# Two encoder layers on one core: the Fourier branch on even and odd halves, gates and branch products with channels on partitions, h scaled ahead of its transposes, tokens in natural order

## The chip, the cores and the metric

The kernel runs on one core of a Trainium2 chip. The metric is the device time of one execution in microseconds. The core has a matrix engine (TensorE, PE), a vector engine (DVE), a scalar engine (ACT), GpSimd (POOL), a queue engine for transfers (SyncE, SP), a 128-partition on-chip memory (SBUF) and eight accumulation banks (PSUM).

## The reference

Two layers, 512 tokens (a grid of 8 rows by 64 columns), 1024 channels. The change lies in the mixer.

```python
for l in range(2):
    x = x + 0.5 * swiglu(rms_norm(x, ffn1_norm[l]), ffn1_w_in[l], ffn1_w_out[l])
    x = x + mixer(rms_norm(x, mix_norm[l]), ...)
    x = x + 0.5 * swiglu(rms_norm(x, ffn2_norm[l]), ffn2_w_in[l], ffn2_w_out[l])
return rms_norm(x, final_norm)

def fourier_mix(u):        # (B, T, 512): 4 groups of 128 channels
    ug = u.astype(jnp.float32).reshape(B, T, 4, 128)
    f = jnp.fft.fft2(ug, axes=(1, 3), norm="ortho").real
    return f.reshape(B, T, 512).astype(u.dtype)

def mixer(h, w_in, gate_bias, rpb, w_na_out, w_f_out, w_o):
    q, k, v, uf, ga, gf = split(h @ w_in)          # 512, 512, 512, 512, 1024, 1024 columns
    y_na = neighbourhood_attention(q, k, v, rpb) @ w_na_out
    y_f = fourier_mix(uf) @ w_f_out
    g_na = jax.nn.sigmoid(ga + gate_bias[0])
    g_f = jax.nn.sigmoid(gf + gate_bias[1])
    return (g_na * y_na + g_f * y_f) @ w_o
```

The attention has 8 heads of 64. A query sees all 8 grid rows and a window of 16 columns, with a learned bias by relative row and column.

## The kernel before

**Precision.** Each fp32 operand of a product is split into a rounded high part (ACT, `S.activation ... Copy`) and the rest as a low part (DVE, a subtraction), and each product is three matmuls, high x high, high x low, low x high (`mm3`). Weights come from DRAM as granules of 128 x 1024 (512 KB) into a raw tile, and are split by `Item.prep` into two rings of three buffers, `whi` and `wlo`. `Stream` holds their order: it fetches `FETCH` = 8 items ahead of the one split, and splits two ahead of the one used (`AHEAD`). A combination of two granules is made by a DMA that adds (POOL's queue, L152, L179) or by DVE (L170). During the first part of the mixer, raw tiles come from the general pool `k` of 23 slots of 4 KB per partition, which also holds nearly everything else (`slot`, `hilo`). Later, raw tiles are nine buffers in the space that the mixer's own pool (`tmp`, `bm`, tables) leaves (`swap_pools`).

**The two FFNs** and the last product of the mixer use one level of Strassen's scheme (seven products for eight). They don't change, but for the tail of the first FFN, where `quad` of the next norm transposes x for the mixer, four blocks of 256 tokens x 512 channels.

**The mixer.** h enters unscaled: x is transposed, multiplied by the norm's gain and split; the reciprocal root r of each token is applied to what comes out of the products. For q and k, where tokens lie along the columns, r is spread over all partitions through DRAM (`R`, `spread`) and multiplied in (L832). Tokens are stored in blocks of 8 grid columns, so that attention's key bands are contiguous.

1. `proj_U`: u for the tokens 0 to 255 and, from a reversed copy (`flip`), for 511 down to 256; sums and differences `ue` of both. 96 + 96 matmuls of 512 columns with `proj_V`.
2. `four_pos`: position DFT of even and odd parts, 48 matmuls of 256 columns, then a rotation by `rot` on DVE. `four_ch`: channel DFT, 24 matmuls. Between them q and k of the first pair of heads.
3. Attention in ten `att_step`s: scores of step i, transposes of i-1, output of i-2; the projections of the later heads between them. `bias_for` builds the bias of a head pair from `rpb` windows and a mask on POOL.
4. `f_rows`: y_f for 128 tokens x 512 channels a time, `rows_of(yf, ...)`, between the last attention steps: 8 tiles of 12 matmuls of 512 columns; ACT empties PSUM.
5. `fill(o, ns, 0, w)`: the same for attention's output, first half of the channels. Then `gate_block(0)` and `gate_block(1)`, each a Strassen product of h with two gate matrices (7 x 24 matmuls of 512 columns), tokens on partitions; `arg` multiplies by r and adds the bias (L1075), a tanh stands for the sigmoid. `to_channels` transposes the gated sums (L1154). `merge` takes the second half of attention's output.
6. The last product with `w_o`, and the squares and transposes for the next norm.

**Order.** The program order is the priority. A list scheduler at build time orders each engine's instructions by it and by modelled readiness; inside `manual_schedule` DVE and ACT keep the written order.

## Time and profile before

| | |
|---|---|
| median of 3 runs | 1945.97 us (1944.67 to 1946.43) |
| the profiled execution | 1945.96 us, span 1944.2 us |
| granted TensorE clock | 0.996 |
| instructions | 24536 |
| moved by DMA | 361.82 MB, mean 186 GB/s |

A line of a group view names the source line, engine, operation, what is written from what, the shape, and the count; after the bar come busy us, mean ns of one, and the engine's idle time just before, with what ended it. A timeline line is start, duration, engine, line, operation. A stage row is the length, then busy time of PE, weight loads (PEld), DVE, ACT and POOL with counts in brackets, the granted clock, DMA share and GB/s. Matmuls are pipelined, so their durations overlap. The line of a helper such as `mm3` (L282 to L284) or `split` (L288 to L291) stands for many places; the names of the tiles tell them apart.

### The profile page before, as it was taken

Reading aid. Unit: us, or ns where it says so; the run is one execution under the profiler, and the core shown is the slowest. Engines: PE = TensorE matmul, PEld = TensorE weight load, DVE = VectorE, ACT = ScalarE, POOL = GpSimd, SP = SyncE. Lnnn points to the kernel's source line nnn. Section 1 sums busy time; section 2 is a strip of 40 time slices with the busy share of each in tenths; the row PEclk is TensorE's granted clock in tenths of the full one; section 3 lists DMA queues with packets and bytes.
Section 4 is the critical chain, followed back from the end, with each engine's and each line's share of the span. In section 5 each row is a group of like instructions: output and inputs, shape, how many; then the busy total and the mean of one; then the engine's idle time right before and its main releaser. Section 6 shows DMA issues by size and latency. Waiting matters only on the chain.

```text
span 1944.2 us, 24536 instructions
## 1 busy us (share of the span) xinstructions
PE 1914.1 (98%) x8997; PEld 1585.1 (82%) x8997; DVE 1569.7 (81%) x1887; ACT 1131.9 (58%) x1606; POOL 201.4 (10%) x246
## 2 busy tenths in 40 slices
PE   9999999999999999999999999999999999999997
PEld 7888888888778888888888888888787888888886
DVE  7767799588788867779967778996878887777898
ACT  6655666355556655566655566653565566555654
POOL 0101010300111010001000100102101110010010
PEclk9999999999999999999999999999999999999999
DMA  8777499321997577749857765965039974776593
GB/s 284 202 201 191 149 254 305 108 57 53 262 220 199 135 187 206 182 152 263 241 141 209 179 172 175 280 231 147 17 99 249 234 191 129 209 181 173 174 280 125
DMA packets 105016, 361.82 MB, mean 186 GB/s; under 512 B 11968, under 2 KB 14144, under 8 KB 104896
## 3 DMA queue, kind: packets, MB, share of 16 engines
q1 hardware_dynamic: 77280, 265.59, 39.2%
q0 software_dynamic: 27328, 94.39, 26.5%
q8 instruction: 70, 1.15, 0.2%
q14 instruction: 50, 0.41, 0.1%
q10 hardware_dynamic: 288, 0.29, 0.0%
HBM read 354.97 MB, written 2.10 MB: 184 GB/s over the span
## 4 chain that ended last, share of the span: by engine, by line
PE 80%; DVE 12%; DMA 3%; issue 3%; ACT 3%; POOL 0%; ACTq 0%; DVEq 0%; POOLq 0%
PE A L282 8%; PE A L284 8%; PE A L283 8%; PE o L283 5%; PE o L284 4%; PE o L282 4%; PE B L283 4%; PE B L284 4%; PE B L282 4%; PE ps L282 4%; PE ps L283 4%; PE ps L284 4%; DVE wlo L289 3%; DMA raw<-in_wst_dram 3%; PE C L283 2%
## 5 line engine op out<-in xcount | busy, mean ns | idle before, releaser
L289 DVE TENSOR_TENSOR wlo<-raw,whi 128x1024 fp32r<-128x1024 f32 (+1 forms) x522 | 623.8, 1200 | 299.7 <-ACT whi L288 299.0
L288 ACT ACTIVATE whi<-raw 128x1024 fp32r<-128x1024 f32 (+1 forms) x522 | 540.1, 1038 | 478.6 <-PE A L284 125.9
L152 POOL DMA_DIRECT2D raw<-in_wst_dram x152 | 131.2, 871 | 1346.9 <-DMA raw<-in_wst_dram 784.9
L283 PE MATMUL A<-wlo,xh 128*128 128x512 f32 x384 | 150.1, 391 | 3.5 <-DVE wlo L173 2.3
L170 DVE TENSOR_TENSOR raw<-raw,raw 128x1024 f32<-128x1024 f32 (+1 forms) x128 | 150.9, 1188 | 2.5
L284 PE MATMUL A<-whi,xl 128*128 128x512 f32 x384 | 149.5, 389 | 0.0
L282 PE MATMUL A<-whi,xh 128*128 128x512 f32 x384 | 149.3, 390 | 0.0
L172 ACT ACTIVATE whi<-raw 128x1024 fp32r<-128x1024 f32 x76 | 78.9, 1039 | 66.6 <-PE B L284 33.2
L173 DVE SCALAR_TENSOR_TENSOR wlo<-raw,whi 128x1024 fp32r<-128x1024 f32 x76 | 90.3, 1194 | 17.0 <-ACT whi L172 17.0
L283 PEld LDWEIGHTS A<-wlo,xh 128*128 128x128 f32 x384 | 72.1, 188 | 20.9 <-DVE wlo L173 4.0
L282 PEld LDWEIGHTS A<-whi,xh 128*128 128x128 f32 x384 | 71.9, 188 | 15.8 <-ACT whi L172 0.8
L284 PEld LDWEIGHTS A<-whi,xl 128*128 128x128 f32 x384 | 72.1, 188 | 14.8
L469 ACT ACTIVATE sn<-A 128x512 f32<-128x512 f32 x96 | 56.8, 599 | 42.0 <-PE A L284 41.9
L282 PE MATMUL B<-whi,t1h 128*128 128x512 f32 x192 | 76.0, 398 | 0.4 <-ACT whi L288 0.4
L282 PE MATMUL A<-whi,t3h 128*128 128x512 f32 x192 | 75.1, 391 | 1.1 <-ACT sn L469 1.1
L283 PE MATMUL B<-wlo,xh 128*128 128x512 f32 x192 | 75.0, 390 | 1.0 <-DVE wlo L289 1.0
L283 PE MATMUL A<-wlo,t2h 128*128 128x512 f32 x192 | 74.8, 390 | 0.5 <-DVE wlo L289 0.5
L283 PE MATMUL C<-wlo,xh 128*128 128x512 f32 x192 | 74.8, 390 | 0.5 <-DVE wlo L289 0.5
L283 PE MATMUL B<-wlo,t1h 128*128 128x512 f32 x192 | 75.0, 391 | 0.2
L282 PE MATMUL C<-whi,xh 128*128 128x512 f32 x192 | 74.8, 391 | 0.2 <-ACT whi L288 0.2
L282 PE MATMUL A<-whi,t2h 128*128 128x512 f32 x192 | 74.9, 392 | 0.0
L282 PE MATMUL B<-whi,xh 128*128 128x512 f32 x192 | 74.8, 390 | 0.0
(348 smaller groups left out, 4882.4 us busy)
## 6 DMA issues: line engine op xcount, KB each, us to landing
raw<-in_wst_dram SPq DMA_DIRECT2D x463, 512.0 KB
raw<-in_wst_dram POOLq DMA_DIRECT2D x168, 512.0 KB, 8.0
raw<-in_wst_dram SPq DMA_DIRECT2D x30, 256.0 KB
vs<-v SPq DMA_DIRECT2D x12, 256.0 KB
bw<-in_rpb_dram SPq DMA_DIRECT2D x32, 68.0 KB
x<-in_xin_dram SPq DMA_DIRECT2D x4, 512.0 KB
raw<-in_wst_dram POOLq DMA_DIRECT2D x8, 256.0 KB, 7.6
dft<-in_dft_dram POOLq DMA_DIRECT2D x8, 256.0 KB, 5.6
```

The source lines that it names most:

```text
L152: G.dma_start(out=self.t, in_=wst[GRAN_AT[self.plus]][:, 0 : self.n], accum_op=ALU.add)
L170: V.tensor_tensor(t, t, self.add.t, ALU.add)
L172: S.activation(hi, t, AF.Copy, scale=-1.0)
L173: V.scalar_tensor_tensor(lo, t, -1.0, hi.bitcast(F32), ALU.mult, ALU.subtract)
L282: PE.matmul(ps, lh, rh, start=start, stop=False, skip_group_check=again)
L283: PE.matmul(ps, lh, rl, start=False, stop=False, skip_group_check=again)
L284: PE.matmul(ps, ll, rh, start=False, stop=stop, skip_group_check=again)
L288: S.activation(hi, src, AF.Copy)
L289: return V.tensor_tensor(lo, src, hi.bitcast(F32), ALU.subtract)
L469: S.activation(t[:, b, :], ps[b], AF.Copy)
```

## The change

- *h scaled ahead.* `Norm.scale` takes the reciprocal root of 256 tokens as soon as their squares are there and writes x times r into `xn`; `quad` transposes that. The late tokens' quads stay in the tail of the first FFN, the early tokens' move into `proj_V`, which now runs first, late tokens first. `R`, `spread`, the reversed root and the multiplications by r are gone.
- *Fourier branch on halves.* `fold` adds and subtracts h of token t and 512 - t. u is projected for 256 folded rows, with the weights folded the same way over channels (adding DMA for the even part, a DVE subtraction for the odd); tokens 0 and 256 and channel 64 are carried as extra rows (`ex`, `ux`, `cx`, `p64`, `w64`). Both DFTs and the output product work on halves, and `f_fill` puts the two halves of y_f together by an addition and a subtraction on DVE, one of them written in reverse.
- *Channels on partitions* for y_f, y_na and the gates (`product_T`, `n_rows`): weights are the stationary side. The gate bias is then an ACT operand, and `to_channels` is gone.
- *Tokens in natural order.* q and k are put into the attention's order when they leave PSUM (`parted`), V goes to DRAM and is read back in bands, the bias comes ready from DRAM (`near`).
- `swap_pools(0)` now follows the last Fourier rows, an Exp is issued before attention, and V's weights keep slots of the general pool (`kept`) until both halves of `proj_V` are done.

```diff
+            if self.kept:
+                hi, lo = slot(F32R, "whi", (1024,))[:, 0:n], slot(F32R, "wlo", (1024,))[:, 0:n]
...
-            for name, n in (("u", 4), ("v", 4), ("qk", 8), ("f", 4)):
-                for g in range(n):
-                    add(Raw((s, name, g)))
+            for g in range(4):
+                add(Raw((s, "v", g)), kept=True)
+            for g in range(3):
+                add(Raw((s, "up", g), UC * len(UK[g]), (s, "uq", g)))
+            for g in range(2):
+                add(Raw((s, "um", g)), Raw((s, "un", g)), op=ALU.subtract)
+            for g in range(8):
+                add(Raw((s, "qk", g)))
+            for i in range(2):
+                add(Raw((s, "fp", i), 1024, (s, "fq", i)))
+                add(Raw((s, "fp", i)), Raw((s, "fq", i)), op=ALU.subtract)
...
+        def scale(self, j):
+            with tc.high_priority():
+                for _ in self.roots(2 * j, 2):
+                    pass
+            for b in range(2):
+                t = self.xn[2 * j + b] = slot(F32, "xn", (D,))
+                for i in range(2):
+                    c = slice(i * T, (i + 1) * T)
+                    S.activation(t[:, c], x[:, 2 * j + b, c], AF.Copy, scale=self.r[:, b : b + 1])
...
+    def product_T(ps, acts, start, again=False):
+        h, l, off = acts
+        for g in range(2):
+            wh, wl = [z.rearrange("p (a b c) -> p a b c", a=2, c=P) for z in ws.next()]
+            for cb in range(4):
+                to = ps[cb // 2][:, cb % 2 * 256 : cb % 2 * 256 + 256]
+                for k in range(2):
+                    kt = 2 * g + k
+                    mh, ml = h[:, kt, off : off + 256], l[:, kt, off : off + 256]
+                    first = start and kt == 0
+                    PE.matmul(to, wh[:, k, cb], mh, start=first and cb % 2 == 0, stop=False, skip_group_check=True)
+                    PE.matmul(to, wh[:, k, cb], ml, start=False, stop=False, skip_group_check=True)
+                    PE.matmul(to, wl[:, k, cb], mh, start=False, stop=kt == 3, skip_group_check=True)
...
         def proj_V():
...
+            def done(c):
                 t = slot(F32R, "v", (2, T))
+                split(t[:, 0, :], t[:, 1, :], pss[c])
+                nc.sync.dma_start(out=vd[c * P : (c + 1) * P].bitcast(F32), in_=t.bitcast(F32))
+            norm.scale(0)
+            pss[2], pss[3] = bank(), bank()
+            for g in range(4):
+                w.append(ws.next())
+                some((2, 3), g)
+                if g in (1, 2):
+                    norm.quad(g - 1, 0)
+            done(2)
+            done(3)
+            fold()
+            pss[0], pss[1] = bank(), bank()
+            for g in range(4):
+                some((0, 1), g)
+            done(0)
+            done(1)
+        def fold():
+            for i in range(2):
+                a, b = norm.raw[i, 0], norm.raw[i, 1]
...
+                t = slot(F32, "ht")
+                V.tensor_tensor(t[:, :, 1:HALF], a[:, :, 1:HALF], b[:, :, HALF - 1 : 0 : -1], ALU.add)
+                V.tensor_copy(t[:, :, 0:1], a[:, :, 0:1])
+                V.tensor_tensor(a[:, :, 1:HALF], a[:, :, 1:HALF], b[:, :, HALF - 1 : 0 : -1], ALU.subtract)
+                for src, to in ((t, hp), (a, hm)):
+                    h, l_ = slot(F32R, "hh"), slot(F32R, "hl")
+                    split(h, l_, src)
+                    to.append((h, l_))
...
-                V.tensor_tensor(s_[e], ps[e], bms[hp][e][:, pr : pr + 2, :].rearrange("p a b -> p (a b)"), ALU.add)
+                V.scalar_tensor_tensor(s_[e], ps[e], DH**-0.5, near_, ALU.mult, ALU.add)
...
+        def f_fill():
+            w64 = slot(F32R, "w64", (1024,))
...
+            V.tensor_tensor(w64[32:36], r64[0:4], w64[0:4].bitcast(F32), ALU.subtract)
+            for i in range(2):
+                (eh, el), (oh, ol) = ws.next(), ws.next()
+                for cb in range(4):
...
+                    pe, po = bank(), bank()
+                    for gp in range(2):
+                        c = slice(gp * T + cb * P, gp * T + cb * P + P)
+                        mm3(pe[:, 0:KC], eh[:, c], el[:, c], pf[gp][:, 0, :], pf[gp][:, 1, :], gp == 0, False)
+                    c = slice(i * T + cb * P, i * T + cb * P + P)
+                    PE.matmul(pe[:, 0:KC], w64[0:68, c], p64[0][0:68, 0:KC], start=False, stop=True)
+                    for gp in range(2):
+                        c = slice(gp * T + cb * P, gp * T + cb * P + P)
+                        mm3(po[:, 0:HALF], oh[:, c], ol[:, c], qf[gp][:, 0, :], qf[gp][:, 1, :], gp == 0, gp == 1)
+                    t = tmp(s="fo")[:, 0:HALF]
+                    S.activation(t, po[:, 0:HALF], AF.Copy)
+                    y = fs[i, cb // 2][:, cb % 2, :]
+                    V.tensor_tensor(y[:, 0:HALF], pe[:, 0:HALF], t, ALU.subtract)
+                    V.tensor_tensor(y[:, T - 1 : HALF : -1], pe[:, 1:HALF], t[:, 1:HALF], ALU.add)
+                    S.activation(y[:, HALF : HALF + 1], pe[:, HALF : HALF + 1], AF.Copy)
+                    yield
...
+        proj_V()
+        for z in range(2):
+            tc.keep_in_program_order(G.dma_start(out=dfs[:, z], in_=dft[z]))
+        tc.keep_in_program_order(G.dma_start(out=fc, in_=four))
+        S.activation(small("tab", 1), ones, AF.Exp)
+        bias_for(0)
+        proj_U()
...
         proj_q(0)
+        four_pos()
         proj_k(0)
+        four_ch()
         proj_q(1)
...
+        f_rows = f_fill()
+        for i, n in ((6, 3), (7, 3), (8, 2)):
+            for _ in range(n):
+                next(f_rows)
             att_step(i)
+        for _ in f_rows:
+            pass
         swap_pools(0)
         att_step(9)
```

More of the change, by code (lines that the diff above doesn't have):

```diff
@@ L695, in stage_ffn @@
             make(i + 2)
-            if i == 6 and not late:
+            if i == 6 and not late and not nxt.mix:
                 nxt.quad(0, 0)
@@ L762, in stage_ffn @@
                 nxt.squares(1, 0)
[L763 removed]
+                if not nxt.mix:
+                    nxt.later((1, 0))
     gf = [None]
@@ L1067, in gate_block @@
-        def gate_block(i, bias, acts, after):
-            r = norm.r
-            def arg(src, which, j):
-                t = src if src is not None else slot(F32, "ga", (2, T))
-                for b in range(2):
-                    c = 2 * j + b
-                    V.scalar_tensor_tensor(
-                        t[:, b, :], pa[b] if src is None else t[:, b, :], r[:, c : c + 1],
-                        bias[which][:, i * T : (i + 1) * T], ALU.mult, ALU.add,
-                    )
-                S.activation(t, t, AF.Tanh, scale=0.5)
-                return t
-            def gated(t, y):
-                V.scalar_tensor_tensor(y, t, 1.0, y, ALU.add, ALU.mult)
-            done = []
+                c = slice(kt % 2 * T + cb * P, kt % 2 * T + cb * P + P)
@@ L1087, in both @@
             def both(j):
[L1089 to L1091 removed]
+                if (i, 0) in ns and gf[j] is not None and ga[j] is not None:
+                    V.tensor_tensor(ga[j], ga[j], gf[j], ALU.add)
             def with_f(t, j):
[L1094 removed]
+                gated(t, fs, j)
+                gf[j] = t
                 both(j)
             def with_n(t, j):
[L1098 to L1102 removed]
@@ L1104, in gate_block @@
-            ga = [None, None]
+                if (i, 0) in ns:
+                    gated(t, ns, j)
+                ga[j] = t
+                both(j)
             for m in ORDER:
```

588 lines of the change are left out of this document (287 added, 301 removed).

## The prediction

> **What bounds the kernel now.** I read the clock and span first, then the page's busy shares, then TensorE's waits, then a table of busy times by stage of the first layer's mixer.
>
> ```profile
> core 0: 1944.2 us, clock 0.996
> PE 1914.1 (98%) x8997; PEld 1585.1 (82%) x8997; DVE 1569.7 (81%) x1887; ACT 1131.9 (58%) x1606; POOL 201.4 (10%) x246
> 340.40:384.90 44.50, 44.50 (x203) 36.96 (x202) 24.49 (x44) 17.12 (x27) 15.10 (x20) 1.00 0.33 102
> 384.90:410.10 25.20, 25.20 (x146) 22.06 (x144) 22.93 (x49) 11.45 (x20) 0.00 (x0) 1.00 0.47 126
> 410.10:457.90 47.80, 45.32 (x281) 37.37 (x280) 43.28 (x74) 28.77 (x70) 9.08 (x12) 1.00 0.06 18
> 457.90:490.60 32.70, 32.70 (x195) 28.13 (x194) 23.84 (x44) 19.54 (x49) 1.76 (x2) 1.00 0.31 110
> 490.60:556.00 65.40, 62.06 (x264) 48.56 (x263) 56.36 (x56) 35.62 (x43) 10.31 (x12) 1.00 0.95 242
> 556.00:627.00 71.00, 71.00 (x334) 59.06 (x333) 59.57 (x64) 41.91 (x51) 8.64 (x10) 1.00 0.83 209
> 1377.00:1425.00 48.00, 45.27 (x260) 36.99 (x259) 40.28 (x71) 27.61 (x69) 9.05 (x12) 0.93 0.06 18
> PE ps L1009 <- ACT s L993: 3.9, 2, 2.1
> ```
>
> The columns of a stage are its length, then busy time of PE, weight loads, DVE, ACT and POOL, the granted clock, the DMA share and GB/s. TensorE is busy 1914.1 of 1944.2 us, so 30 us in all are idle, and a microsecond saved on TensorE counts if nothing else is late. The mixer has stages with different second limits. The projections U and V (340.4 to 384.9) leave DVE nearly half idle. Attention (410.1 to 457.9) has DVE at 43.28 of 47.80 and TensorE idle for 2.48 us. The Fourier output rows with the last attention steps (457.9 to 490.6) are TensorE's alone, DVE 23.84 of 32.70. The start of the gates (490.6 to 556) has TensorE idle for 3.34 us, with DMA at a share of 0.95 and DVE at 56.36. The second layer's attention shows the same (45.27 of 48.00), so I work out one layer and double it.
>
> **The price of a matmul.**
>
> ```profile
> 385.04 0.28 PE L282 MATMUL ps<-dft,u 128*128 128x256 f32 x1
> 390.67 0.28 PE L284 MATMUL ps<-dft,u 128*128 128x256 f32 x1
> 390.79 0.40 PE L282 MATMUL ps<-xh,whi 128*128 128x512 f32 x1
> 394.67 0.39 PE L284 MATMUL ps<-xh,wlo 128*128 128x512 f32 x1
> 401.47 0.39 PE L284 MATMUL ps<-xh,wlo 128*128 128x512 f32 x1
> 327.86 1.75 PE tr L363 x16
> L284 PEld LDWEIGHTS ps<-dft,u x32: 187/192/192, 385.2 to 1352.2; 128*128 128x128 f32 x32
> ```
>
> Durations overlap, so I go by start to start. The 48 position-DFT matmuls of 256 columns fill 385.04 to 390.79: 0.120 us each. Thirty matmuls of 512 columns fill 394.67 to 401.47: 0.2267 each. A narrow one thus costs 0.53 of a wide one. 16 transposes take 1.75 us: 0.109 each. For 258 and 260 columns I take 0.120 too (the two rows give 0.0004 us a column).
>
> **TensorE's sum for one layer**, with counts from the loops (three products per fp32 pair). Projection of u: 96 wide become 64 of 260 columns (eight tiles times 2 x 3, plus 2 for the middle tokens) and 48 of 256: 21.76 to 13.44, -8.3. Position transform: 48 narrow become 21 + 12: -1.8. Channel transform: 24 become 19: -0.6. The mirrored reciprocal's matmul goes: -0.2. Fourier rows: 8 times 12 wide become 8 times 13 narrow: 21.76 to 12.48, -9.3. Gates: 336 wide become 672 narrow: 76.2 to 80.6, +4.4. The transposes of the gated result go, 32 of them: -3.5. The V projection, q and k, attention, attention output rows, merge and last product keep their counts. Sum: -19.3 us per layer, -38.6 for both. That is the most TensorE can give.
>
> The gate term is where a rule speaks against the change: half-length matmuls double the weight loads. The load rows are 0.192 us long, longer than the 0.120 us between starts, with a new load for each of the 48, so loads are hidden under earlier matmuls there and I add nothing for them.
> The Trainium skill, page "TensorE: Matmul & The Clock Gate", section "Measured speedup vs the span model", states that a weight load overlaps matmuls in flight only when its row group differs, and its section "LDWEIGHTS (loading the stationary operand)" gives 107 ns for 128 columns. By that rule 336 further loads would add an estimated 36 us per layer; the rows here, at full height throughout, disagree.
>
> **DVE, ACT and the stages in which they decide.**
>
> ```profile
> L832 DVE TENSOR_TENSOR q<-ps,R 128x512 f32<-128x512 f32 x16 | 11.0, 688 | 9.0 <-PE ps L284 9.0
> L1075 DVE SCALAR_TENSOR_TENSOR sn<-sn,r,gb 128x512 f32<-128x512 f32 x24 | 16.9, 743 | 0.0
> L289 DVE TENSOR_TENSOR wlo<-raw,whi 128x1024 fp32r<-128x1024 f32 x494 | 605.1, 1230 | 299.7 <-ACT whi L288 299.0
> 389.01 0.42 DVE L912 TENSOR_TENSOR bt<-m,m 128x256 f32<-128x256 f32 x1
> 389.34 0.42 DVE L913 TENSOR_TENSOR bt<-m,m 128x256 f32<-128x256 f32 x1
> 468.03 1.28 DVE L986 TENSOR_TENSOR s<-ps,bm 128x512 f32<-128x512 f32 x2
> 471.07 0.17 DVE L996 RECIPROCAL rs<-sm 128x2 f32<-128x2 f32 x1 [0.57 <-ACT s L993]
> 415.13 1.28 ACT L993 ACT_TABLE_LOAD   x1 [3.48 <-DVE nmx L987]
> ```
>
> A DVE operation on 256 columns takes DVE 0.34 us (389.01 to 389.34), on 512 about 0.6 (two in 1.28), on 1024 about 1.2.
>
> *Attention.* The multiplication of q and k by R goes: five of the eight lie here, 5 x 0.6 = 3.0 us of DVE. The Fourier weights add one subtraction of 1.2. The new Exp ahead of attention takes the table load (1.28 us) off the chain at 415 us, where TensorE waited some 2 us (3.9 in both layers, the longest 2.1). The bias is loaded whole instead of being added on POOL; POOL's adds hide beside DVE, so nothing is taken for them. Each of TensorE's idle causes here is reduced and 2.48 us is all there is: I take -2.0.
>
> *Fourier rows.* TensorE falls from 32.7 to 23.4. DVE did 23.84 with ACT alone emptying PSUM. It now gets 16 operations of 256 columns (8 x 2 x 0.34 = 5.4), a subtraction (1.2) and the row of channel 64 (a 1024-column subtraction on four partitions; bounds 0.3 and 1.2 by the 256- and the 1024-column rows; I take 1.2, since work goes by columns): 31.6. Three attention steps each wait 0.57 for the exponentials, 1.7 more. So DVE takes over as the bound at some 31 us, some of which can be done before or after: I take -2 rather than -9.3 (ends 0 and -9.3).
>
> *Gates.* Sixteen multiply-adds with r and bias go (16 x 0.66 = 10.6 of DVE). Tanh reads 256 columns at a time with the bias as ACT operand. That is DVE relief of 10 us in a stage at 56.36 of 65.40, but the DMA share there is 0.95. TensorE gives +4.4 - 3.5 = +0.9, and I take 1 of the 3.34 idle as regained: 0 (ends +2 and -3).
>
> **What the scaling ahead adds at the front.**
>
> ```profile
> 326.37 0.63 ACT L328 ACTIVATE junk<-x 128x512 bf16<-128x512 f32 x1 [0.40 <-DVE x L598]
> 343.15 0.16 DVE L398 TENSOR_TENSOR ms<-ssq 128x4 f32<-128x4 f32 x1
> 345.82 0.17 DVE L308 SCALAR_TENSOR_TENSOR r<-rt,r 128x4 f32<-128x4 f32 x1
> 340.36 0.39 PE L282 MATMUL ps<-whi,xh 128*128 128x512 f32 x1
> L369 ACT ACTIVATE xr<-tr,gn 128x256 f32<-128x256 f32 x48 | 18.8, 472 | 0.0
> L288 ACT ACTIVATE xh<-xr 128x1024 fp32r<-128x1024 f32 x16 | 17.1, 1070 | 11.4 <-DVE xr L540 11.3
> vs<-v SPq DMA_DIRECT2D x12, 256.0 KB
> raw<-in_wst_dram POOLq DMA_DIRECT2D x168, 512.0 KB, 8.0
> 461.15 24.23 SPq L150 DMA_DIRECT2D raw<-in_wst_dram  x7
> ```
>
> Transposes of the late tokens start at 327.9 now, right after x. They will wait for the squares (to 327.0), the reciprocal root (343.15 to 345.99, 2.8) and four scalings of 512 columns (as the squares, 0.63 each, 2.5): 332.3. Then come eight copies at 0.47, two splits at 1.07 and a low part at 1.2: 339.4, or 342.6 if three weight splits of 1.07 go between. The mixer's first matmul, at 340.36 now, is due at 339.5 because a quad's transposes (0.9) move behind it. Stall 0 to 3; I take 1.5. The early tokens' scaling follows the last x update and is covered by the 48 wide matmuls of the late tokens (10.9 us), which come first. Then the folding: per half two 1024-column sums, two splits, about 4.8 us of DVE, needed when proj_U begins, 10.9 us after the second half of V. All of it hides there if buffers are free. But V's weights now hold 8 of 23 slots until that half is used up, raw weights some 9, transposed h 4, V's tiles 2: folding gets its first slots after a quarter of the half (2.7 us) or when V's store lands (8.0 us by POOL's row, the nearest for 512 KB). First need 2.7 + 4.8 = 7.5 of 10.9: no stall. By 8.0: 12.8, 1.9 stall. I take 2.0 (ends 0 and 6, folding only after the whole half). V's fourteen reads back from DRAM replace twelve copies and are first needed two attention steps later; on SP's queue they stand ahead of later q/k weights, which are prefetched eight items deep: nothing taken, and 8.0 if a weight comes behind them. Next stage's weights start on SP at 461.15, long before their use, and now some earlier since the DFT tables' space is free sooner: 0.
>
> Front: -8.3 - 1.8 - 0.6 - 0.2 + 1.5 + 2.0 = -7.4.
>
> **Sum.** -7.4 - 2.0 - 2.0 + 0 = -11.4 per layer, -22.8 in all. The profiled execution took 1945.96 us, its span 1944.2 with 1.8 around it; the median is 1945.97, so they are the same. 1945.96 - 22.8 = 1923.
>
> **Rivals.**
>
> *DVE is no limit.* The Fourier rows' additions are done beside TensorE, and the front has no stall: -19.3 and the table load's -1.3, 2 x -20.6, 1905. For it: the 8.9 us that DVE is idle between 457.9 and 490.6. Against: DVE is also full before and after, so nothing can be put off. Chance 0.22.
>
> *The front gives nothing.* The fold waits for all of V's second half and its DMA, 7.4 us more than I took per layer: -4.0, 1938. For it: the slot count. Against: slots come free in quarters. Chance 0.18.
>
> *Slower: the slot pool runs dry.* Weights for U, q and k cannot be fetched while slots are held. Each such miss costs TensorE a landing (8.0) and a split (1.07 + 1.2): 10.3 us. From the 11.4 saved, two misses per layer give 9.2 us too many: 1964; it decides from 1.1 misses per layer. Against: the projections of U and V have a DMA share of 0.33, no TensorE gap (44.50 of 44.50), and fetches run eight items ahead. Chance 0.06.
>
> *Slower: loads not hidden in the gates.* If a narrow gate matmul took its load's 0.192 instead of 0.120, 672 x 0.072 = 48 us per layer: 2 x (48 - 11.4), 2019; it decides from 0.137 us a matmul. Against: the 48 rows above. Chance 0.02.
> The rule of "TensorE: Matmul & The Clock Gate" on overlap would lead here.
>
> **How the numbers follow.** Forecast 1923, chance 0.52 (its own range 1912 to 1932). The range from 1903 to 1940 takes in the first two rivals and leaves out the slower ones and 0.1 of the tails. A measurement here tells about 0.2%, 3.9 us, from no change. Faster: 0.52 + 0.22 + most of 0.18 = 0.89; same 0.04; slower 0.07.
>
> **What would show it.** Right: 672 gate matmuls at 0.12 us start to start; U in 112 matmuls and 13.4 us; no table load on the chain at the first exponentials; DVE over 95% busy in the Fourier rows, with TensorE idle there 5 us or more; one or two TensorE gaps of 1 to 3 us at the mixer's start and before proj_U. Wrong: TensorE full through the Fourier rows (then 1905), gaps over 5 us behind weights in the projections (then 1938 or slower), or gate matmuls above 0.13 us.

## The result, and the profile after

The changed kernel takes 1972.55 us (median of four runs, 1967.59 to 1978.72) where the kernel before takes 1945.32: a ratio of 1.0146, 95% interval [1.0112, 1.0179], so it is slower by some 27 us. A second set of six runs, e14 below, gave 1972.34 and a ratio of 1.0142 [1.0119, 1.0166]. The forecast was 1923 and faster; it was wrong in size and in sign.

First the clock and the busy shares of the changed kernel (profiled execution of 1967.59 us), then its table by stage of the first layer's mixer (columns as in the prediction), then what TensorE waited for, over both layers (total, times, longest). Line numbers have moved: L293 to L295 are the three products, L299 and L300 the ACT and the DVE half of a split, L1042 to L1058 the softmax and its transposes.

```profile
core 0: 1965.6 us, clock 0.984
PE 1900.5 (97%) x9609; PEld 1599.7 (81%) x9609; DVE 1539.6 (78%) x1842; ACT 1149.6 (58%) x1684; POOL 169.4 (9%) x204
```

```profile
340.20:352.40 12.20, 2.20 (x17) 1.71 (x16) 7.61 (x19) 10.80 (x22) 0.00 (x0) 0.76 1.07 326
352.40:391.80 39.40, 39.38 (x225) 34.11 (x226) 27.36 (x31) 23.27 (x38) 0.34 (x1) 0.94 0.45 159
391.80:424.00 32.20, 29.73 (x140) 22.94 (x139) 12.11 (x19) 9.93 (x20) 1.41 (x2) 0.89 0.75 212
424.00:472.00 48.00, 47.89 (x306) 40.85 (x305) 43.48 (x75) 30.73 (x75) 0.95 (x1) 1.00 0.15 48
472.00:499.30 27.30, 21.47 (x161) 18.54 (x160) 22.60 (x51) 16.27 (x52) 0.00 (x0) 0.95 0.14 49
499.30:560.00 60.70, 59.80 (x430) 56.58 (x431) 49.83 (x50) 35.70 (x52) 11.22 (x13) 0.96 0.96 260
560.00:632.00 72.00, 70.49 (x449) 63.45 (x449) 54.51 (x62) 39.97 (x54) 9.53 (x11) 1.00 0.83 210
```

```profile
PE ps L293 <- ACT xh L299: 15.5, 2, 8.6
PE ps L1058 <- DVE rs L1045: 5.3, 4, 1.4
PE ps L981 <- ACT ce L299: 3.4, 2, 1.7
PE ps L1058 <- ACT s L1042: 3.4, 1, 3.4
...
PE tr L375 <- ACT xn L390: 2.9, 2, 1.5
PE ps L293 <- ACT whi L299: 2.8, 2, 1.4
```

Two things are new. Between 340.2 and 352.4 TensorE does 2.20 us of work; and the granted clock, 1.00 in every stage of the first layer before, is below 1.00 in five of these seven. TensorE is busy 13.6 us less than before (1914.1 to 1900.5), though its work was to shrink by 38.6. The lost clock accounts for most of the difference: (1 - 0.984) x 1965.6 = 31.4 us against (1 - 0.996) x 1944.2 = 7.8, so 23.6 us more (an upper estimate, since the low clock also covers idle time). 13.6 + 23.6 = 37.2. A second estimate comes from e15 below, whose clock is 0.996 as before: TensorE is busy 1891.1 us there, about 9 of them with 84 added filler matmuls (50 such take 5.62 us in e4), so some 32 less than before. Most of the work that the change was to remove is gone. In the changed kernel the time was spent on waiting (65.1 us idle, 30.1 before) and on running at half clock.

The same by milestones of the first layer, each the start of the first such matmul in the two timelines:

| first matmul of | before | after | difference | forecast to here |
|---|---|---|---|---|
| the projections | 340.36 | 352.42 | +12.1 | +0.6 (339.5 + 1.5) |
| the scores | 410.13 | 422.35 | +12.2 | -7.4 |
| the Fourier rows | 457.92 | 467.03 | +9.1 | -9.4 |
| attention's output rows | 490.55 | 499.37 | +8.8 | -11.4 |
| the next FFN | 638.1 | 648.3 | +10.2 | -11.4 |

The miss is 21.6 us in this layer, and 19.6 of it arises ahead of the scores. The second layer adds nearly as much: the changed kernel reaches its last FFN 19.9 us late (1622.08 against 1602.19).

### The three places

**The mixer's start.** ACT's timeline around the gap (start, length, engine, line, in brackets the idle time before it and what ended it), then TensorE's.

```profile
339.73 0.63 ACT L340 ACTIVATE junk<-x 128x512 bf16<-128x512 f32 x1 [6.52 <-DVE x L618]
340.36 2.54 ACT L390 ACTIVATE xn<-x,r 128x512 f32<-128x512 f32 x4
344.33 0.85 ACT L299 ACTIVATE whi<-raw 128x780 fp32r<-128x780 f32 x1 [0.82 <-DMA raw<-in_wst_dram]
...
350.35 1.07 ACT L299 ACTIVATE whi<-raw 128x1024 fp32r<-128x1024 f32 x1
351.30 1.07 ACT L299 ACTIVATE xh<-xr 128x1024 fp32r<-128x1024 f32 x1
```

```profile
341.73 2.14 PE L375 MATMUL tr<-ident,xn 128*128 128x128 f32 x16 [1.47 <-ACT xn L390]
352.42 0.80 PE L293 MATMUL ps<-whi,xh 128*128 128x512 f32 x1 [8.55 <-ACT xh L299]
```

DVE had the reciprocal root of the late tokens ready at 335.7. ACT stood idle for 6.52 us with the scalings (xn) queued behind the squares of an x update that wasn't there yet; then weight splits, two of them waiting for their DMA (0.82 us, above, and 0.58), stood between the copies and the splits of h. On DVE, the root's thirteen small operations took 7.5 us (from 328.2), not 2.8, because splits of 1.2 us and updates of x stand between the first of them.

**SP's queue and ACT's queue at the channel transform.** SP's issues, then ACT.

```profile
384.55 18.68 SPq L1237 DMA_DIRECT2D vc<-vd  x14
403.96 10.62 SPq L150 DMA_DIRECT2D raw<-in_wst_dram  x5
```

```profile
407.48 1.06 ACT L299 ACTIVATE whi<-raw 128x1024 fp32r<-128x1024 f32 x1 [6.42 <-PE ps L294]
408.44 0.58 ACT L299 ACTIVATE q<-ps 128x512 fp32r<-128x512 f32 x1
408.92 0.65 ACT L299 ACTIVATE ce<-ps 128x258 fp32r<-128x258 f32 x2
```

V's fourteen reads hold SP for 18.7 us, and five weights are issued only behind them. On ACT a weight split waits 6.42 us for its ring buffer, with the copies of q and of the position transform behind it; TensorE waits for the latter (ce, 1.7 us per layer).

**The tail of attention.** From 472.0 to 499.3 TensorE is idle for 5.8 us (27.30 - 21.47), mostly behind reciprocals of the softmax, copies of p and the first weight split of the output rows. The next stage's weights, which SP issued from 461.15 before, come with one exception from 494.3 on.

The table load that the early Exp was to take off the chain is still there, and a second one is at the program's start:

```profile
3.19 1.28 ACT L1226 ACT_TABLE_LOAD   x1
423.80 1.28 ACT L1042 ACT_TABLE_LOAD   x1
```

That Exp reads a constant, so nothing ties it to its place in the program, and it was issued at 3 us. In this layer the load cost nothing: it ended at 425.08, and ACT then waited until 426.97 for DVE's part of the softmax.

### The profile page after: what moved, and what is told of

Same layout as the page of the kernel before. It is cut to its first block, busy times and chain, and to the rows that moved or that the text cites. A ratio compares the mean times of both kernels' runs of the same rounds, so it can differ in the third digit from the quotient of the medians.

```text
span 1965.6 us, 25798 instructions
## 1 busy us (share of the span) xinstructions
PE 1900.5 (97%) x9609; PEld 1599.7 (81%) x9609; DVE 1539.6 (78%) x1842; ACT 1149.6 (58%) x1684; POOL 169.4 (9%) x204
## 4 chain that ended last, share of the span: by engine, by line
PE 67%; DVE 15%; DMA 8%; issue 5%; ACT 4%; SPq 0%; POOL 0%; ACTq 0%; DVEq 0%; POOLq 0%
DMA raw<-in_wst_dram 7%; PE A L293 7%; PE A L294 7%; PE A L295 7%; DVE wlo L300 5%; PE B L293 4%; PE B L295 4%; PE B L294 4%; PE o L294 2%; PE o L295 2%; PE ps L293 2%; PE o L293 2%; PE ps L294 2%; PE ps L295 2%; PE C L294 2%
## 5 line engine op out<-in xcount | busy, mean ns | idle before, releaser
L300 DVE TENSOR_TENSOR wlo<-raw,whi 128x1024 fp32r<-128x1024 f32 (+1 forms) x524 | 619.9, 1189 | 307.6 <-ACT whi L299 305.2
L299 ACT ACTIVATE whi<-raw 128x1024 fp32r<-128x1024 f32 (+1 forms) x524 | 539.4, 1034 | 482.8 <-PE A L295 116.3
L173 DVE TENSOR_TENSOR raw<-raw,raw 128x1024 f32<-128x1024 f32 (+1 forms) x136 | 160.6, 1190 | 17.9 <-DMA raw<-in_wst_dram 15.4
L295 PE MATMUL A<-whi,xl 128*128 128x512 f32 x320 | 124.6, 389 | 0.0
L293 PE MATMUL A<-whi,xh 128*128 128x512 f32 x320 | 124.5, 389 | 0.0
L294 PE MATMUL A<-wlo,xh 128*128 128x512 f32 x320 | 124.5, 389 | 0.0
L295 PEld LDWEIGHTS A<-whi,xl 128*128 128x128 f32 x320 | 60.1, 188 | 12.5
L293 PEld LDWEIGHTS A<-whi,xh 128*128 128x128 f32 x320 | 60.1, 188 | 12.5
L293 PE MATMUL B<-whi,t1h 128*128 128x512 f32 x160 | 63.7, 398 | 0.0
L293 PE MATMUL A<-whi,t3h 128*128 128x512 f32 x160 | 62.4, 390 | 1.3 <-ACT sn L489 1.3
L294 PE MATMUL C<-wlo,xh 128*128 128x512 f32 x160 | 62.4, 390 | 0.5 <-DVE wlo L300 0.5
L295 PE MATMUL B<-whi,t1l 128*128 128x512 f32 x160 | 62.4, 390 | 0.0
L295 PE MATMUL A<-whi,t2l 128*128 128x512 f32 x160 | 62.3, 389 | 0.0
L294 PE MATMUL A<-wlo,t3h 128*128 128x512 f32 x160 | 62.3, 389 | 0.0
L294 PE MATMUL B<-wlo,t1h 128*128 128x512 f32 x160 | 62.3, 389 | 0.0
L295 PE MATMUL C<-whi,xl 128*128 128x512 f32 x160 | 62.3, 389 | 0.0
```

Source lines behind the costliest of these rows:

```text
L173: V.tensor_tensor(t, t, self.add.t, self.op)
L293: PE.matmul(ps, lh, rh, start=start, stop=False, skip_group_check=again)
L294: PE.matmul(ps, lh, rl, start=False, stop=False, skip_group_check=again)
L295: PE.matmul(ps, ll, rh, start=False, stop=stop, skip_group_check=again)
L299: S.activation(hi, src, AF.Copy)
L300: return V.tensor_tensor(lo, src, hi.bitcast(F32), ALU.subtract)
```

## The experiments

Each was timed in five rounds beside the kernel before; ratios are against it. Its median was 1943.9 to 1946.4 in these sets, so times of different sets carry some 2 us besides their own spread.

### One place at a time

**e1_front.** Order on ACT and DVE at the mixer's start.

```
 with manual_schedule(DVE, ACT):
     make(i + 2)
     nxt.scale(1)
+    ws.prep(ws.prepped + 1)      # V's first weight split
     nxt.quad(1, 1)
     nxt.quad(0, 1)
...
+with tc.issue_after(<last split of the quads>):
     nxt.squares(1, 0)            # and the weight splits of proj_V, proj_U
```

> Only the order on ACT and DVE at the mixer's start is changed: the scalings, copies and splits of the late tokens go ahead of the last update's squares and of the weight splits of U, and the first weight split of V goes right behind the scalings. Theory A (in-order queues, and a lower clock behind each gap): of TensorE's 1.47 + 8.55 us of idle per layer about 3 stay, and the ten wide matmuls behind the gap come 0.23 us apart instead of 0.43 (2 us per layer): 2 x (7 + 2) = 18 us less than the changed kernel's 1972.6, so 1954. Theory B (weights or slots come late): the gap stays over 6 us and moves behind a weight split or a DMA, 1965 or more. Theory C (narrow matmuls cost more than 0.120 us): the idle goes as in A, but nothing of the low clock elsewhere, 1958.

1964.49 us, ratio 1.0108 [1.0092, 1.0124]: 8 less, not 18. The first wait went from 8.6 to 5.0 us:

```profile
348.46 0.79 PE L293 MATMUL ps<-whi,xh 128*128 128x512 f32 x1 [4.97 <-ACT xh L301]
```

A wait of 5 us still lowered the clock (the next matmuls came 0.43 us apart), and the wait at the first exponentials (3.4 us in one layer of the changed kernel) is in both now, 4.5 us in all.

**e2_rows.** Weights' memory opened earlier.

```
-for i, n in ((6, 3), (7, 3), (8, 2)):
+for i, n in ((6, 3), (7, 2), (8, 1)):
     ...
-rest of the rows; swap_pools(0); att_step(9)
+swap_pools(0); one row; att_step(9); the last row
```

> The memory for the next stage's weights is opened before the last Fourier rows (after the eighth attention step, with two rows left), the rows' scratch moves to the slot pool, and one row moves from the last steps behind it. Theory A (weights were issued too late): their first issue moves from 494 to some 480 us, the 1.41 us wait for the weight split and the slow matmuls behind it (18 at 0.43 instead of 0.227, 3.5 us) go: 2 x 5 = 10 less, 1963. Theory B (the rows are too short to cover the softmax, the weights do not matter): the gaps of 1.28 and 1.39 us behind the softmax stay or grow, since the step before the last has a row less, and the time stays within 4 us of 1972.6. Theory C (the slots are too few for the scratch): a new wait in the rows, 1975 or more.

1979.07, ratio 1.0164 [1.0143, 1.0185]. Theory B: with a row less in front of each of the last two softmax transposes the waits for the reciprocals grew from 5.3 to 11.3 us, the longest from 1.4 to 3.0. Its time says less, since its profile also has a wait of 9.4 us at the first exponentials, which this edit doesn't touch; e14 below shows such waits without any edit.

**e3_chan.** Order on ACT around the channel transform.

```
-proj_k(0); four_ch(); proj_q(1)
+proj_k(0, weight split behind the copies of four_pos)
+four_ch()
+proj_q(1, weight split behind the copies of four_ch)
```

> Only the order on ACT around the channel transform is changed: the weight splits of the next projections are queued behind the copies of q and of the position and channel transforms. Theory A (ACT waits 6.4 us for a buffer of the weight ring with these copies queued behind): TensorE's waits of 1.68 and 0.8 us at 408 to 412 us go, and the matmuls from 410 to 418 us come 0.12 and 0.227 us apart instead of 0.21 and 0.43 (4.5 us): 2 x 7 = 14 less than 1972.6, 1959. Theory B (the copies wait for free slots, and the weight split only stands first): the same gap under another name, 1970 to 1975.

1975.09, ratio 1.016 [1.0147, 1.0174]: no gain, and neither theory as put. The waits for ce and q went, and a longer one appeared in front of the first softmax. DVE, then TensorE, of e3:

```profile
425.31 1.23 DVE L173 TENSOR_TENSOR raw<-raw,raw 128x1024 f32<-128x1024 f32 x1 [9.48 <-DMA raw<-in_wst_dram]
429.17 1.22 DVE L173 TENSOR_TENSOR raw<-raw,raw 128x1024 f32<-128x1024 f32 x1 [2.63 <-DMA raw<-in_wst_dram]
...
436.12 1.08 PE L1061 MATMUL ps<-ident,s 128*128 128x128 f32 x4 [10.85 <-ACT s L1045]
```

L173 subtracts two raw weights of the Fourier rows. They were not there, and DVE's in-order queue held the split of q and the softmax behind them. The gap at the channel transform had only been first in line; late weights stood behind it. How much of the 10.85 us is due to the edit is open, since e14 has up to 6.7 there without it.

**e4_warm.** Filler in the gap at the start.

```
 nxt.quad(1, 1)
 nxt.quad(0, 1)
+for _ in range(52):
+    PE.matmul(pw[:, 0:256], ident_bf16[:, 0:128], ident_bf16)
```

> 52 matmuls of 256 bf16 columns on the identity, whose product nobody reads, stand behind the transposes at the mixer's start, about 6 us, in the gap of 8.55 us. Nothing else is changed. Theory A (a gap lowers the clock for the work behind it): the gap's end stays at 352 us, the granted clock from 350 to 360 us rises from 0.66 to over 0.9, and the ten wide matmuls behind come 0.23 us apart: 2 x 2 to 2 x 4 us less, 1965 to 1969. Theory B (the matmuls behind the gap are slow because their operands come late): they stay at 0.43, 1972.

1961.16, ratio 1.0085 [1.0071, 1.0099], more of a gain than theory A's 1965 to 1969. The two layers differ. In the first the filler ended early, and 3.3 us of idle were left; the clock fell. In the second 1.4 us were left, and it held. The second layer's start, changed kernel and then e4:

```profile
1305.00:1330.00 25.00, 16.62 (x71) 12.94 (x70) 15.28 (x30) 17.50 (x31) 0.00 (x0) 0.80 0.67 250
```

```profile
1305.00:1330.00 25.00, 21.89 (x138) 18.04 (x137) 16.01 (x27) 20.70 (x38) 0.00 (x0) 1.00 0.57 214
```

Theory A for the clock: it is the gap, not late operands, that doubles the distance of the matmuls behind it.

### SP's queue

**e5_chan_v** and **e16_v_only.** The reads of V are moved; e5 has e3's order on ACT as well, e16 nothing else.

```
-proj_U(); <14 reads vc<-vd>; proj_q(0); four_pos(); ... proj_q(1)
+proj_U(); proj_q(0); four_pos(); ... proj_q(1); <14 reads vc<-vd>
```

> The order of e3, and the fourteen reads of V from DRAM moved behind the second q projection, so that on SP's queue the later weights of q, k and the Fourier rows stand ahead of them. Theory A (the reads hold SP's queue for 20 us, so five weights are issued late; DVE's subtraction of the Fourier weights waits for them with the first softmax queued behind): the wait of 10.8 us in front of the first exponentials goes, and with it some 3 us of slow matmuls: 2 x 8 to 2 x 13 less than e3's 1975, 1949 to 1959. Theory B (DMA as a whole is too slow there, share 0.6 to 1.0): the same bytes arrive as late, V's tiles instead of weights, and a wait of 5 to 10 us stands in front of the first attention output; 1970 to 1980.

> The changed kernel with only the fourteen reads of V moved behind the second q projection; ACT's order is not pinned. Theory A (SP's queue is the cause, ACT's order follows from late weights): most of e5's gain over the changed kernel (16 us) is here, 1956 to 1962. Theory B (both must go, since the copies of q and of the transforms still stand behind a weight split): 1965 to 1972.

1956.16 (1.0060 [1.0048, 1.0072]) and 1956.38 (1.0051 [1.0038, 1.0063]). The move alone gives the whole 16 us, 8 per layer on average (of the 11 us between the two profiled runs, 2 lie in the first layer and 9 in the second); ACT's order adds nothing to it. SP's issues of e16, against the two rows above:

```profile
383.71 16.93 SPq L150 DMA_DIRECT2D raw<-in_wst_dram  x6
400.82 3.35 SPq L1242 DMA_DIRECT2D vc<-vd  x5
```

The waits at the first exponentials, for ce and for q left e16's list of TensorE's waits; in their place stand four waits for copies of p, 4.8 us in all, at most 1.9 at a time.

### The front and the tail, on top of e5

**e6_front_q**, still on the changed kernel, with e1's order: the half that V reads first is transposed first.

```
-nxt.quad(1, 1); nxt.quad(0, 1)
+nxt.quad(0, 1); nxt.quad(1, 1)
```

> As e1, and of the late tokens the channels that the first V matmuls read are transposed first (the other half was first before). Theory A (TensorE waits for the chain of scaling, transposing, copying and splitting): the first V matmul starts about 2.5 us earlier, at 346 us, the gap falls from 4.97 to 2.5 us: 2 x 2.5 = 5 less than e1's 1964.5, 1959.5; if the gap is then short enough to keep the clock, a further 2 x 2.5, 1954. Theory B (the gap's end is set by the V weights): it stays at 348.4, 1964.

1966.37 (1955.17 to 1974.69), ratio 1.0117 [1.0091, 1.0143]. The wait at the start fell to 1.8 us, more than expected, and the time didn't follow: TensorE now waited up to 4.5 us for the early tokens' scaling and up to 4.2 at the first exponentials. A shorter front reached the next wait sooner.

**e7_rows_one.** One row in front of the tenth step.

```
-for i, n in ((6, 3), (7, 3), (8, 2)):
+for i, n in ((6, 2), (7, 3), (8, 2)):   # the last row before att_step(9)
```

> One of the Fourier rows moves from in front of the seventh attention step to in front of the tenth, where no row stood; nothing else. Theory A (the rows are too short to cover the softmax): the waits of 1.28 and 1.39 us in front of the transposes stay, and those of 0.5 to 1 us in all in front of the last attention output go, -2 x 0.5 to -2 x 1.5: 1970 to 1972. If the last weights are what counts, they are issued 1.5 us later against the end of the rows or as before: 1972 to 1974.

1978.16, ratio 1.0168 [1.015, 1.0185]: no gain. Inconclusive for the rows, since its profile, like e2's, has the late weights (9.5 us at the first exponentials).

**e8_together.** e5, e6, e7, and the Exp tied to its place.

```
-S.activation(small("tab", 1), ones, AF.Exp)
+tc.keep_in_program_order(S.activation(small("tab", 1), ones, AF.Exp))
```

> e6, e5 and e7 in one, and the small Exp that was to load the table early is held at its place in the program (in the changed kernel it ran at 3 us). If the waits are separate places that add up: 1972.6 - 13 (e6) - 14 (e5) - 1 (e7) - 2 (the table) = 1943, about as the kernel before. If a wait removed at one place returns at the next, as from e3's channel transform to the first softmax: 1955 or more.

1954.54, ratio 1.0054 [1.0042, 1.0066]: as e5 alone, so the front's gain came back elsewhere. Where, TensorE's timeline of e8 shows:

```profile
353.57 2.98 PE L378 MATMUL tr<-ident,xn 128*128 128x128 f32 x11 [4.89 <-ACT xn L393]
```

The early tokens' transposes stand in TensorE's queue after half of V's first 48 matmuls, and their scaling wasn't done.

**e9_front.** That, mended, on top of e5 and e6's order.

```
 for g in range(4):
     some((2, 3), g)
-    if g in (1, 2): norm.quad(g - 1, 0)
+for i in range(2): norm.quad(i, 0)
+# the weight splits of proj_V and proj_U behind the last operation of the root on DVE
```

> On top of e5: the front's order of e6, and the early tokens' transposes are moved behind all four weight groups of V's first half (they stood in TensorE's queue ahead of the last two, which do not need them), and the reciprocal root of the early tokens goes ahead of U's weight splits on DVE. Theory A (queue positions make the front's idle): the idle behind the scalings (4.9 us in e8) and the gap at the start (8.9 in e5, 1.8 in e8) fall to 2 to 4 us in all per layer, and the matmuls behind the start keep 0.227: 1956 - 2 x (10.4 - 3) - 2 x 2 = 1937. Theory B (the work of scaling, copying and splitting is too long for its cover wherever it stands): 6 us or more stay in front of V's second half, 1948 or more.

1944.25, ratio 1.0002 [0.9993, 1.0011]: 12 us from e5. Three short waits are left in the front:

```profile
342.86 0.50 PE L293 MATMUL ps<-whi,xh 128*128 128x512 f32 x1 [1.76 <-ACT xh L301]
344.12 0.59 PE L295 MATMUL ps<-whi,xl 128*128 128x512 f32 x1 [0.53 <-DVE xl L302]
...
354.98 0.50 PE L294 MATMUL ps<-wlo,xh 128*128 128x512 f32 x1 [1.50 <-DVE wlo L302]
```

**e12_unscaled.** e5 without the scaling and its root, so that the mixer gets an h that isn't normed.

```
-src = self.xn[2 * j + b] if self.mix else x[:, 2 * j + b, :]
+src = x[:, 2 * j + b, :]
```

> On top of e5: x is transposed as it is; the mixer's scaling by the reciprocal root is left out, with the root itself. Theory A (the front's idle is the price of scaling ahead of the transposes): idle of 1.5 + 8.9 us and 2 us of slow matmuls per layer go, 1956 - 24 = 1932; what stays is the copying and splitting, at most 3 us of idle. Theory B (V's weights, whose splits stand in the same queue, set the start): the gap stays at 5 us or more and the time at 1945 or more.

1945.2, ratio 1.0012 [1.0003, 1.0022]: the time of theory B, with a gap of 4.5 us where B said 5. Without any scaling the start still had this wait behind the split of xh, because squares and a weight split stood ahead of it on ACT:

```profile
346.50 0.80 PE L293 MATMUL ps<-whi,xh 128*128 128x512 f32 x1 [4.53 <-ACT xh L301]
```

e9, which scales and has the queues in order, is as fast. So most of the cost was not the scaling as such but its place in three in-order queues. What an unscaled kernel in e9's order would take was not run.

**e10_tail** and **e17_n_early.** On top of e5. e17 has the second edit alone.

```
-proj_k(0); four_ch(); proj_q(1)          # four_pos() stood in front
+proj_k(0); proj_q(1)
...
+four_pos(); four_ch()
-for i, n in ((6, 3), (7, 3), (8, 2)):
+for i, n in ((6, 0), (7, 3), (8, 3)):

+for g in range(2): add(Raw((s, "n", 0, g)))   # still the mixer's stage
 st += 1
-for g in range(2): add(Raw((s, "n", 0, g)))
```

> On top of e5: position and channel transform (52 narrow matmuls, about 6.3 us) move from in front of attention to in front of its seventh step, three Fourier rows each stand before the eighth and ninth and two before the tenth, and the first two weights of the attention's output belong to the mixer's own loads. Theory A (the tail is too short of matmuls to cover the softmax, and its weights come late): the waits of 5.3 (softmax), 4.8 and 2.1 (last split) and 2.8 us (weight split) in the two layers fall to 4 in all, and the slow matmuls at 495 to 505 us go: 1956 - 11 - 5 = 1940. Theory B (DVE is the bound there, so the same waits come at other steps): 1953 to 1958.

> e5, and only the first two weights of the attention's output rows are loaded and split with the mixer's own weights; the position and channel transforms stay in front of attention. Theory A (the tail's loss is its late weights): most of e10's gain over e5 (7 us), 1948 to 1951. Theory B (it is the missing cover of the softmax): 1954 to 1956, and the waits of 5.3 us behind the reciprocals stay.

e10: 1948.81, ratio 1.0025 [1.0014, 1.0036], 7 less than e5 instead of 16. e17: 1960.04, ratio 1.0068 [1.0055, 1.0082], no gain over e5 and outside both of its theories. Its wait of 1.4 us for the first weight split is gone, but the waits behind the softmax grew from 5.3 us to this:

```profile
PE ps L1061 <- ACT s L1045: 9.4, 4, 3.3
```

So the first weights' early arrival doesn't help by itself, and the tail's loss was at least in part missing cover for the softmax, which e10's first edit gives (that edit alone was not run). e10's other half is lost behind it: TensorE waits 3.9 us (longest 2.3) for weight splits at the start of the gates.

**e11_both.** e9, e10 and the tied Exp.

> e9 and e10 in one, and the small Exp held at its place. If the two places are separate, the gains add: 1956 - 19 - 16 - 2 = 1919, faster than the kernel before by 1.3% and near the forecast for the change. If one returns at the other (the tail's work comes earlier into weights not yet there): 1935 or more.

1937.89, ratio 0.9967 [0.9955, 0.9979]: faster than the kernel before, by 6 us, and 15 short of the forecast. Its clock and busy shares, and the waits of its list that are its own:

```profile
core 0: 1936.8 us, clock 0.991
PE 1888.9 (98%) x9609; PEld 1596.0 (82%) x9609; DVE 1540.6 (80%) x1842; ACT 1147.3 (59%) x1682; POOL 169.8 (9%) x204
```

```profile
PE B L474 <- ACT whi L301: 4.3, 3, 1.8
PE ps L1070 <- DVE rs L1057: 4.1, 2, 2.1
```

In the first layer it reaches the output rows at 482.19, 8.4 us ahead of the kernel before, and the next FFN at 635.9, only 2.2 ahead. The other 6.2 us are lost in the gates. From 500 to 520 and from 520 to 540 the granted clock is 0.93 and 0.91 there, 1.00 before; in e15 below it is 1.00, and output rows and gates take 150.5 us instead of 153.7. So about half of the loss goes with the clock. The rest may be late weights: the first of them are issued from 483.7 (from 461.15 before), and the DMA share from 500 to 520, 1.00 in both kernels, leaves no room to catch up; no run tested it.

### The clock's share

**e13_warm_all**, **e14_after**, **e15_both_warm.** Filler as in e4 in all three gaps of the changed kernel; the changed kernel itself; e11 with filler in its three longest gaps.

> The changed kernel with matmuls on the identity, whose product nobody reads, in its three gaps: 70 at the mixer's start (8.4 us), 20 in front of the channel transform, 10 each in front of the last two softmax transposes and 12 in front of the attention's output rows. No wait is changed. Theory A (half of the loss is the low clock behind gaps, 31.4 us of lost clock after against 7.8 before): the mean granted clock rises from 0.984 to 0.993 or more and the time falls by 12 to 20 us, 1953 to 1961; TensorE's idle that is left plus the filler stays at some 65 us. Theory B (the waits alone cost, the clock only marks them): no change, 1970 to 1976, since the filler ends before what is waited for.

> The changed kernel itself, for a base on the same chip and in the same rounds: 1972.6 as in its first four runs, within 1968 to 1979.

> e11 with 14 such matmuls each in three gaps that it has left: at the mixer's start (1.8 us), in front of the first attention output (1.9) and in front of the transposes of the eighth attention step (2.1). If those gaps of 2 us lower the clock: 0.991 to 0.994 and 3 to 6 us less than e11's 1937.9, 1932 to 1935. If gaps of 2 us don't: no change, 1937 to 1939.

e13: 1966.59, ratio 1.0117 [1.0098, 1.0135], 6 us less than e14's 1972.34; the clock rose from 0.980 to 0.992 in the profiled runs. Half of what A expected, and e13's waits say why:

```profile
PE ps L1065 <- ACT s L1049: 14.1, 2, 9.5
```

The matmuls at full clock reached the late Fourier weights sooner and waited there. e4, with filler in the first gap alone, had gained 11, so the clock's share is known only to lie at some 6 to 11 us. e14's profiled run, one of 1979.91 us, has the same wait without any edit (10.5 us in two, longest 6.7), behind this:

```profile
428.58 1.23 DVE L173 TENSOR_TENSOR raw<-raw,raw 128x1024 f32<-128x1024 f32 x1 [10.85 <-DMA raw<-in_wst_dram]
```

The profiled run of 1967.59 shows the 3.4 us in one layer only. These weights are thus also where, at least in part, the changed kernel's runs differ by up to 17 us (1962.83 to 1979.91): 7.1 us between these two profiled runs, which are 12.3 apart; e16, with the reads moved, stays within 1954.34 to 1959.26.

e15: 1935.34, ratio 0.9953 [0.9937, 0.9969], with the clock at 0.996. It is the fastest here, though its interval overlaps e11's; a gain of 2.6 us from keeping the clock over gaps of 2 us isn't settled.

## Why the prediction was wrong

- **TensorE's sum** (-38.6) held for the most part: 32 to 37 by the estimates above. The price held too. Here are the first and the last of 23 matmuls of the gates in a row:

```profile
549.13 0.28 PE L471 MATMUL A<-xh,whi 128*128 128x256 f32 x1
...
551.77 0.28 PE L472 MATMUL A<-xl,whi 128*128 128x256 f32 x1
```

  22 distances in 2.64 us are 0.120 each, each with a weight load of its own. The rival of loads not hidden is excluded: the loads are at full height, 0.192 us long, and hidden.
  The rule of the Trainium skill, page "TensorE: Matmul & The Clock Gate", section "The mechanism" (a load overlaps only where the row group differs; the prediction names the section behind it), does not hold here.
- **Attention** (-2.0) came out at -3.1 between the first score and the first Fourier row of the first layer, and at -0.2 in the second (50.94 us against 51.13), where the first exponentials were waited for 3.4 us. That the first layer came out near was partly luck. The step that named the table load failed (the Exp ran at 3 us); what went there was DVE's work, 43.30 to 40.15 us busy.
- **Fourier rows** (-2, ends 0 and -9.3) came out at -0.3, within the ends but by another mechanism: DVE was busy for 22.60 of 27.30 us, not over 95%. TensorE's idle of over 5 us, which was to show that DVE is the bound, came all the same (5.8), so that sign was met by luck. The rows became too short to cover the softmax, which the prediction had counted as three waits of 0.57.
- **Gates** (0, ends +2 and -3) came out at +1.4.
- **The front** (-7.4) is the step that failed: +12.2 at the first score. Three terms of it were mis-sized or missing.
  - "Stall 0 to 3; I take 1.5" for the start: TensorE sat idle for 1.47 + 8.55 = 10.0 us, and its first matmul came 12.1 later than before. The chain was summed as if each engine took it up at once, with three weight splits as the worst case. On ACT it stood behind squares of a later update and among weight splits that waited for their DMA, on DVE the first root operations stood behind splits and updates. Likewise "the early tokens' scaling ... is covered by the 48 wide matmuls": their transposes stood after 24 of them, which cost nothing while the start was late and up to 4.9 us once it was early (e6, e8). Setting these in order gave 12 us in all (e5 to e9).
  - V's reads on SP's queue: "nothing taken, and 8.0 if a weight comes behind them". Five weights came behind them, and moving the reads gave 16 us, 8 per layer (e16). The bound was priced and then set aside because weights are prefetched eight deep; but the prefetch goes through the same queue. That 8.0 and 8 agree is chance: 8.0 was the landing time of one DMA, and here the queue was held for 18.7 us.
  - The clock had no term. The profile before showed 1.00 in every stage of the first layer, but 0.93 in the second layer's attention, a row that the prediction shows and reads only for its busy times. There a wait of 2.07 us is followed by matmuls 0.427 us apart, in the kernel before:

```profile
1380.49 1.00 PE L1009 MATMUL ps<-ident,s 128*128 128x128 f32 x4 [2.07 <-ACT s L993]
...
1385.57 0.63 PE L284 MATMUL ps<-xh,wlo 128*128 128x512 f32 x1
1386.00 0.63 PE L282 MATMUL ps<-xh,whi 128*128 128x512 f32 x1
```

- **The rivals.** "The slot pool runs dry" (1964, chance 0.06) was nearest in time and right that weights come late; but what made them late was their place on SP behind the reads, since the same weights came in time when that alone was changed.

Step by step the gains are 16 (reads), 12 (front) and 6 us (tail and table, e9 to e11), 34 from 1972 to e11's 1938. The steps were taken one on top of the other, so that sum is e11 by construction. That they are separate places has one test: on e5, the front alone gave 12 and the tail alone 7, and both with the tied Exp 18. Of the 15 us that are left to 1923, the first layer's gates hold 6.2, half of it with the clock; why the rest is missing was not tried.

## What to carry to other kernels

When a change makes TensorE's work shorter, read for each operation of a new chain what is queued ahead of it on its own engine, and for each new DMA what is queued behind it; the durations alone gave a stall of 1.5 us here where TensorE sat idle for 10. Where the trace before shows a prefetch that is always in time, ask whether the new transfers share its queue, and keep the price if they do. Waits hide one another, so the gain of mending one shows only when the next one in line is gone too (e3 and e6 against e5 and e9).

## What the hardware showed that was not expected

Behind a wait of 3.3 us or more TensorE ran at half clock: 512-column matmuls 0.427 us apart instead of 0.227 (353.01, 353.44, 353.87 in the changed kernel), for 4.5 us there, 6.3 in e4's first layer and 7.7 behind e13's wait of 4.6. Shorter waits did it sometimes. One of 2.07 did in the kernel before (0.66 granted from 1380 to 1390 us), and one of 1.79 in its first layer did not (1.00 from 415 to 425). Waits of 1.3 to 1.8 us mostly did nothing (484.07 in the changed kernel, the start in e8), but e11's start with waits of 1.76 and 0.53 close together shows 0.83 in its ten microseconds. In the changed kernel's tail, five waits of 1.39, 0.37, 0.47, 0.34 and 0.20 us between 491 and 497 left 0.60 from 496 to 500, and the output rows at 499.37 came at 0.43.
The Trainium skill, page "TensorE: Matmul & The Clock Gate", section "What's actually happening", states that the clock falls to 1.2 GHz after an idle window of some 3.4 us and returns after as long of sustained work, in windows that run freely. The distance agrees (512 columns at 1.2 GHz are 0.427 us); the wait of 2.07 us is shorter than that window and lowered the clock all the same, and the clock took 4.5 to 7.7 us to return.
